# Hybrid sparse and window attention block on one core: division and lower parts on TensorE in the window branch, a new step order in the sparse branch, counting in both, mix from the first half

## The chip, the core and the metric

The kernel runs on one core of a Trainium2 chip, in one launch. The metric is the device time of that core in microseconds (us). Three runs of the kernel before give a median of 1457.87 us. The engines are TensorE (PE in the profile; PEld is its weight load), VectorE (DVE), ScalarE (ACT), GpSimd (POOL) and SyncE (SP), whose queue issues the DMAs.

## The reference

A decoder block over 1024 positions of width 1024, in float32. Two attention branches work on the same normalised input and are mixed by gates; an MLP follows.

```python
h = rmsnorm(x, attn_norm_w)
a_q, a_k, a_v, i_q, i_k, i_w, b_q, b_k, b_v, g_a, g_b = split(h @ w_in)
# a: sparse branch, per block of 128 queries
score = sum_h i_w[t,h] * relu(i_q[t,h] . i_k[s])        # 8 index heads, causal
sel   = top_k(score, 256)                                # 256 keys for each query
o_a   = softmax(a_q . a_k[sel] / 8) @ a_v[sel]           # 8 heads in 2 groups
# b: window branch, keys t-127..t, with one sink logit per head
o_b   = softmax([b_q . b_k / 8, sink])[:-1] @ b_v
mix = sigmoid(g_a) * (o_a @ w_branch_a) + sigmoid(g_b) * (o_b @ w_branch_b)
x = x + mix @ w_out
u = relu(rmsnorm(x) @ w_up); x = x + (u * u) @ w_down
out = rmsnorm(x)
```

## The kernel before

**Split products.** Every product whose operands have to be exact to float32 is made of three products of rounded operands: `mm3` (lines 110 to 115) multiplies upper by upper, upper by lower and lower by upper part. `split` (99 to 108) makes the parts: the upper one is a rounding copy (line 103 on ScalarE), the lower one the difference of source and upper part (line 108 on VectorE or GpSimd).

**Stages.** The program loads the input, begins the first gates, projects index keys and values, and computes the index scores of the blocks 2 to 7 (the blocks 0 and 1 have no more than 256 keys, so nothing is selected there). Then come the window branch `b`, the sparse branch `a`, the mix of both (`attended`, `mixed`), the product with `w_out` (tiles `pso`) and the MLP (tiles `pu`, `pdx`, `pdy`) as fast matrix products of seven block products each.

**A step** is one head group (of two, four heads each) and one block of 128 queries. Each branch has sixteen. A window step has the keys of its block and of the one before, 256 columns (128 in block 0); a sparse step of block n has all 128(n+1) columns, masked by the selection (`bias`). `attention_parts` (819 to 896) runs a step in two halves of two heads. `scores`: two products per head into a bank `S` of 512 columns (line 835; there are two banks), VectorE adds the mask and takes the row's maximum (851), ScalarE makes the exponential and its sum (854), VectorE the reciprocal of the sum (858), and then the probabilities are divided: by VectorE in the window branch (866), by GpSimd in the sparse branch (862). `apply`: for each pair of key blocks, four transposes by TensorE into a bank `pt` (877, three banks), then `split` into upper and lower part (103 on ScalarE, 108 on VectorE), then two products for each key block into the bank `pv` (882 with the upper, 883 with the lower part). At the end ScalarE copies `pv` out (890) and two stores go to DRAM (894) through SP's queue.

**Queries.** `Unit` projects the queries of a pair of blocks (tiles `mm`, lines 112 to 114, 256 columns; two times 24 products), rotates them (440, 441) and rounds them (403, 455). The four query weights are loaded and split ahead by `Columns`, on GpSimd.

**Counting.** The 256th largest score of a query is found by bisection over the bits of its float: in each round every query's row is counted against a candidate, and the candidate's next bit follows. ScalarE counts the blocks 2 to 4 (`below`, 676; VectorE compares and sets the bits, 739 to 742), VectorE the blocks 5 to 7 (674, and 736, 737 with GpSimd's 735). `bits(kind, n)` issues n rounds, `thresholds` the last one. `select(b)` (766 to 780) then makes the mask of block b. In the window branch each step ends with one round of ScalarE and two of VectorE (`RATE`, lines 923 to 928); what is left of both comes before the first sparse step.

**What sets the order.** The lines are written in a software pipeline (`pipeline`, from 466): the second half of a step's work is written `DEPTH` parts behind the first, projections `AHEAD` of it. The gates are fillers: `FILL` says for every step of a stage how many half gates (24 products of 512 columns into tiles `gt` with the copy 291 to `z_d`) are written behind it. A scheduler (`schedule_with_timeline_sim`) then sets the order of each engine's instructions. `A_ORDER` gives the order of blocks of the sparse branch: group 0 takes 1, 0, 5, 4, 7, 3, 6, 2, then group 1 takes 6, 7, 5, 0, 4, 1, 3, 2. The probabilities of a step lie in a `Ring` (`pB`, `pA`), and a step isn't begun before its place is free.

**Mix.** `attended(half, brs)` (954 to 964) loads a half of the positions of a branch's output (first the last stores, `ZLATE`), adds its two parts and splits; `mixed(half, ft, ...)` (967 to 988) loads the gates, makes the sigmoid and multiplies (975 to 985). The second half of the positions is mixed first, the first half `SKEW` = 2 tiles behind.

## Time and profile before

| | |
|---|---|
| median of 3 runs | 1457.87 us (1457.07 to 1458.74) |
| profiled execution | 1457.79 us, span 1455.9 us |
| TensorE busy | 1373.5 us (94%) |
| VectorE busy | 1072.9 us (74%) |
| ScalarE busy | 783.0 us (54%) |
| GpSimd busy | 450.9 us (31%) |
| granted TensorE clock, mean | 0.987 |

The span is the time from the first to the last instruction in the trace; the rest of the profiled execution's time lies around it. Busy time is the time in which an engine had at least one instruction under way. TensorE's instructions overlap, so a busy stretch of it can hold more or fewer products. The shares are means over stages with different limits: the index stage ends at 237 us, the window branch lies from there to 433, the sparse branch to 621, the mix to 741 and the rest behind it.

### The profile page before, as it was taken

The page shows a single profiled execution, that of the slowest core. Times are in us where ns is not written, and L with a number is a line of the kernel's source. Part 1 is how long each engine was busy: PE and PEld are TensorE (multiplying, and loading weights), DVE is VectorE, ACT ScalarE, POOL GpSimd, SP SyncE. Part 2 cuts the span into 40 slices and gives each one's busy share as a digit, 9 for nine tenths or more (in the row PEclk, how much of TensorE's full clock was granted, in tenths as well). Part 3 has the DMA queues.
Part 4 walks back from the last instruction along what each step waited for, and adds up shares of the span by engine and source line. Part 5 has one row for each costly group of instructions (what it writes and reads, how often), then busy time and mean ns, then how long its engine had stood idle before and what let it go on. Part 6 is the DMA issues. An engine that isn't in the chain of part 4 may idle for free.

```text
span 1455.9 us, 21190 instructions
## 1 busy us (share of the span) xinstructions
PE 1373.5 (94%) x7096; PEld 1164.7 (80%) x7096; DVE 1072.9 (74%) x2115; ACT 783.0 (54%) x1612; POOL 450.9 (31%) x447
## 2 busy tenths in 40 slices
PE   7999997888789899979999999999999999999998
PEld 6998886767688788867788878888888888888887
DVE  8667799999998984887553686566664697687674
ACT  6335445666676474864445576555554554445453
POOL 4463766564647554443525310000000000001001
PEclk9999998999999999999999999999999999999999
DMA  7321232232323022185556466444443988632313
GB/s 266 111 70 52 64 116 64 74 90 51 96 61 86 23 54 63 45 258 197 166 146 195 126 207 210 142 149 151 157 147 108 332 285 286 224 102 87 123 59 116
DMA packets 135245, 195.04 MB, mean 134 GB/s; under 512 B 15968, under 2 KB 59104, under 8 KB 135008
## 3 DMA queue, kind: packets, MB, share of 16 engines
q1 hardware_dynamic: 134992, 193.69, 41.7%
q8 instruction: 56, 0.92, 0.3%
q14 instruction: 53, 0.43, 0.1%
q10 hardware_dynamic: 144, 0.00, 0.0%
HBM read 130.99 MB, written 55.84 MB: 128 GB/s over the span
## 4 chain that ended last, share of the span: by engine, by line
PE 59%; DVE 23%; DMA 7%; issue 4%; ACT 4%; POOL 2%; SPq 1%; DVEq 0%; ACTq 0%; POOLq 0%
DVE of_a L674 7%; PE pu L1112 7%; PE pu L1113 7%; PE pu L1114 7%; PE pdx L1311 3%; PE pdx L1309 3%; PE pdx L1310 3%; PE pdy L1309 2%; PE pdy L1311 2%; PE pdy L1310 2%; DVE wide L851 2%; PE pso L112 2%; PE pso L113 2%; PE pso L114 2%; PE S L835 2%
## 5 line engine op out<-in xcount | busy, mean ns | idle before, releaser
L1256 POOL TENSOR_TENSOR y<-x,gf 128x512 f32<-128x512 f32 x4 | 6.3, 1604 | 493.8 <-DVE x L1240 493.8
L103 ACT ACTIVATE dao<-da 128x512 fp32r<-128x512 f32 x112 | 69.8, 630 | 126.1 <-PE pdx L1311 61.7
L112 PE MATMUL mm<-of_h,of_w 128*128 128x256 f32 x416 | 120.4, 291 | 0.0
L113 PE MATMUL mm<-of_h,of_w 128*128 128x256 f32 x416 | 119.6, 289 | 0.0
L114 PE MATMUL mm<-of_h,of_w 128*128 128x256 f32 x416 | 119.5, 289 | 0.0
L854 ACT ACTIVATE wide<-wide,of_a 128x257 f32<-128x257 f32 (+9 forms) x128 | 81.0, 634 | 65.4 <-DVE of_a L851 64.4
L108 DVE TENSOR_TENSOR dao<-da,dao 128x512 fp32r<-128x512 f32 x112 | 77.3, 695 | 40.7 <-ACT dao L103 40.7
L674 DVE TENSOR_SCALAR_CACHE_REDUCE of_a<-wide,of_a 128x768 bf16<-128x768 bf16 (+5 forms) x93 | 106.1, 1141 | 0.9
L1112 PE MATMUL pu<-XT,uo 128*128 128x512 f32 x256 | 99.9, 390 | 0.8 <-ACT snap L1145 0.8
L1113 PE MATMUL pu<-XT,uo 128*128 128x512 f32 x256 | 99.7, 390 | 0.0
L1114 PE MATMUL pu<-XT,uo 128*128 128x512 f32 x256 | 99.5, 389 | 0.0
L112 PE MATMUL gt<-of_h 128*128 128x512 f32 x224 | 91.2, 407 | 7.0 <-ACT of_h L334 7.0
L1310 PE MATMUL pdx<-dbo,dao 128*128 128x512 f32 x248 | 95.5, 390 | 0.0
L1309 PE MATMUL pdx<-dbo,dao 128*128 128x512 f32 x248 | 95.5, 390 | 0.0
L1311 PE MATMUL pdx<-dbo,dao 128*128 128x512 f32 x248 | 94.0, 390 | 0.5 <-DVE dao L108 0.5
L676 ACT ACTIVATE of_a<-uall,of_a 128x384 int8<-128x384 f32 (+2 forms) x93 | 66.8, 718 | 51.2 <-DVE of_a L742 31.4
L835 PE MATMUL S<-of_w 128*128 128x256 f32 (+3 forms) x320 | 79.8, 342 | 14.9 <-DVE of_a L851 14.8
L114 PE MATMUL gt<-of_h 128*128 128x512 f32 x224 | 91.2, 408 | 2.4 <-POOL of_h L108 2.4
L113 PE MATMUL gt<-of_h 128*128 128x512 f32 x224 | 91.1, 407 | 0.9 <-DVE of_h L335 0.9
L877 PE MATMUL pt<-kept,wide 128*128 128x128 f32 x408 | 68.4, 278 | 17.8 <-DVE wide L866 8.8
L113 PEld LDWEIGHTS mm<-of_h,of_w 128*128 128x128 f32 x416 | 81.9, 197 | 1.0
L112 PEld LDWEIGHTS mm<-of_h,of_w 128*128 128x128 f32 x416 | 81.7, 197 | 0.8
(284 smaller groups left out, 4298.4 us busy)
## 6 DMA issues: line engine op xcount, KB each, us to landing
u_d<-u SPq DMA_DIRECT2D x112, 256.0 KB, 2.2
da<-u_d SPq DMA_DIRECT2D x112, 256.0 KB, 4.5
ur<-in_w_up_dram SPq DMA_DIRECT2D x32, 512.0 KB, 4.7
dr<-in_w_down_dram SPq DMA_DIRECT2D x64, 256.0 KB, 5.3
z_d<-of_g SPq DMA_DIRECT2D x32, 256.0 KB, 2.2
uall<-z_d SPq DMA_DIRECT2D x32, 256.0 KB, 3.5
raw<-in_w_out_dram SPq DMA_DIRECT2D x32, 256.0 KB, 4.5
of_g<-in_w_g_dram SPq DMA_DIRECT2D x28, 256.0 KB, 2.8
```

The lines of the kernel that those rows point to most:

```text
L112: ins = nc.tensor.matmul(ps, lhsT=ah, rhs=bh, start=first, stop=False)
L113: nc.tensor.matmul(ps, lhsT=ah, rhs=bl, start=False, stop=False)
L114: nc.tensor.matmul(ps, lhsT=al, rhs=bh, start=False, stop=last)
L674: nc.vector.tensor_scalar(j, src, c, None, op0=ALU.is_lt, op1=ALU.add, accum_out=a)
L835: marks["S"] = nc.tensor.matmul(pS[:, :e - c], lhsT=st.unit(b, j), rhs=kT[:, a, k0 + c:k0 + e], start=a == 0, stop=a == 1).ins
L854: nc.scalar.activation(pe, pe, AF.Exp, bias=last, scale=-1.0, accum_out=st.sm[:, j:j + 1])
L1112: nc.tensor.matmul(ps, lhsT=ah, rhs=xh[:, at], start=f0, stop=False, skip_group_check=True)
L1113: nc.tensor.matmul(ps, lhsT=ah, rhs=xl[:, at], start=False, stop=False, skip_group_check=True)
L1114: nc.tensor.matmul(ps, lhsT=al, rhs=xh[:, at], start=False, stop=last, skip_group_check=True)
L1309: nc.tensor.matmul(ps, lhsT=ah[:, js], rhs=x[0][:, at], start=first, stop=False, skip_group_check=True)
L1310: nc.tensor.matmul(ps, lhsT=ah[:, js], rhs=x[1][:, at], start=False, stop=False, skip_group_check=True)
L1311: nc.tensor.matmul(ps, lhsT=al[:, js], rhs=x[0][:, at], start=False, stop=end, skip_group_check=True)
```

## The change

*Window branch.* The division by the sum leaves the probabilities: the loop of line 862 to 866 runs for the sparse branch alone. The output is multiplied instead: for each of the four heads TensorE transposes the reciprocal, broadcast along the row, into a bank `rb`, and VectorE multiplies the copied output by it. The lower part of the transposed probabilities is made by TensorE and ScalarE: behind the transposes in bank `pt` ScalarE copies the upper part out, TensorE adds to the bank the product of the upper part with the negative identity (`minus`), and ScalarE copies out what is left, the lower part.

*Sparse branch.* The order of the steps is a list of (group, block): it begins with the blocks 1, 0, 3, 2 of group 0, goes through all eight of group 1 and ends with 6, 7, 5, 4 of group 0. The query weight of group 0 is loaded and split a second time for the last four steps. VectorE's rounds of counting alternate between two and one in the window steps, and eight more rounds are written into the first seven sparse steps. `select` comes at the first use of a block, from the step ahead. The ring of the sparse branch ends ahead of `topall`, which VectorE's counting still reads, until the last step is begun.

*Mix.* The first half of the positions is mixed first, the second half behind it. The buffers for it lie in another part of `uall`. *Fillers:* `FILL` has other numbers of half gates per step.

```diff
-FILL = {'i': '000000000000', 'b': '0222000000010110', 'a': '1101110011011111'}
+FILL = {'i': '000000000000', 'b': '0222011001010101', 'a': '1111011010101010'}
...
-A_ORDER = [[1, 0, 5, 4, 7, 3, 6, 2], [6, 7, 5, 0, 4, 1, 3, 2]]
+A_STEPS = [(0, 1), (0, 0), (0, 3), (0, 2), (1, 1), (1, 0), (1, 3), (1, 2), (1, 5), (1, 4), (1, 7), (1, 6), (0, 6), (0, 7), (0, 5), (0, 4)]
+BITS = {'b': '2121212121212121', 'a': '1111112'}
...
     ident = kept(P)
     make_identity(nc, ident)
+    minus = const.tile([P, P], F32R, name="minus")
+    nc.vector.tensor_scalar(minus, ident, -1.0, None, op0=ALU.mult)
...
             nc.vector.reciprocal(inv, inv)
-            for j in range(j0, j0 + 2):
+            for j in range(j0, j0 + 2) if st.name == "a" else ():
...
                 ph, pl = att["ph"](), att["pl"]()
-                split(ph[:, :m], pl[:, :m], pt[:, :m], "act")
+                if st.name == "b":
+
+                    nc.scalar.copy(ph[:, :m], pt[:, :m])
+                    nc.tensor.matmul(pt[:, :m], lhsT=minus, rhs=ph[:, :m], start=False, stop=True, skip_group_check=True)
+                    nc.scalar.copy(pl[:, :m], pt[:, :m])
+                else:
+                    split(ph[:, :m], pl[:, :m], pt[:, :m], "act")
...
-            if EVAC == "a":
+            if st.name == "b":
+
+                rb = bank("tr", [P, R, P], "rb")
+                for j in range(R):
+                    nc.tensor.transpose(rb[:, j], st.sm[:, j:j + 1].to_broadcast([P, P]), ident)
+                nc.scalar.copy(o, st.pv)
+                nc.vector.tensor_tensor(o, o, rb, ALU.mult)
+            elif EVAC == "a":
                 nc.scalar.copy(o, st.pv)
...
         bits("act", RATE["act"])
-        bits("dve", RATE["dve"])
+        bits("dve", int(BITS['b'][i]))
...
-    pA = Ring(wide)
+    pA = Ring(wide, wide_spent)
+    more = Columns(I["w_aq"][0], 2, 256, "pool", "pool", tag="p")
+    steps = [Step(g, b, more if i >= 12 else wq[2 + g], kT=akT[g], v=av[g], kb=(0, b + 1), sink=False, p=pA, dst=o_d["a"],
...
     bits("act", RATE["a"] - done["act"])
-    bits("dve", 32)
...
     def begin(i):
+        if i == NB:
+            pA.end = wide.shape[1]
         if i:
             bits("act", RATE["late"])
-        if i == 0 and steps[0].b in IDX_BLOCKS:
-            select(steps[0].b)
-        if i + 1 < NB and steps[i + 1].b in IDX_BLOCKS:
-            select(steps[i + 1].b)
+        bits("dve", int(BITS['a'][i:i + 1] or 0))
+        for st in steps[i:i + 2]:
+            if st.b not in ready:
+                ready.add(st.b)
+                select(st.b)
...
-    attended(1, "ba")
-    attended(0, "b")
+    attended(0, "ba")
+    attended(1, "b")
...
-            mixed(1, i, *ws[i])
+            mixed(0, i, *ws[i])
         if i == 0:
-            attended(0, "a")
+            attended(1, "a")
         if i >= SKEW:
-            mixed(0, i - SKEW, *ws[i - SKEW])
+            mixed(1, i - SKEW, *ws[i - SKEW])
```

What stands on the engines, at three places. First TensorE in the ninth window step, before. `gt` are gate products (lines 112 to 114), `pt` transposes (877), `S` scores (835), `pv` products with the values (882).

```order
L114 MATMUL gt<-of_h 128x512
L112 MATMUL gt<-of_h 128x512
L877 MATMUL pt<-kept,wide 128x128
L113 MATMUL gt<-of_h 128x512
L877 MATMUL pt<-kept,wide 128x128 x3
L114 MATMUL gt<-of_h 128x512
L112 MATMUL gt<-of_h 128x512
L113 MATMUL gt<-of_h 128x512
L835 MATMUL S<-of_w 128x128
L882 MATMUL pv<-of_w 128x256
L835 MATMUL S<-of_w 128x128 x3
```

TensorE in the same step, after. Scores are line 839 now, transposes 881, the products with the negative identity 886, products with the values 892 and 893, and 903 are the transposes of the reciprocal.

```order
L839 MATMUL S<-of_w 128x128 x4
L886 MATMUL pt<-of_w,minus 128x512
L881 MATMUL pt<-kept,wide 128x128 x4
L839 MATMUL S<-of_w 128x128 x4
L893 MATMUL pv<-of_w 128x256
L892 MATMUL pv<-of_w 128x256
L893 MATMUL pv<-of_w 128x256
L892 MATMUL pv<-of_w 128x256
L881 MATMUL pt<-kept,wide 128x128 x4
L903 MATMUL rb<-kept,of_a 128x128 x4
```

The gate products are gone from this step, and the new product (886) and the four transposes of the reciprocal (903) stand between scores and products with the values.

Second, TensorE among the large blocks of the sparse branch, before (block 5 of group 1).

```order
L835 MATMUL S<-of_w 128x256 x2
L877 MATMUL pt<-kept,wide 128x128 x3
L883 MATMUL pv<-of_w 128x256
L882 MATMUL pv<-of_w 128x256
L883 MATMUL pv<-of_w 128x256
L882 MATMUL pv<-of_w 128x256
L877 MATMUL pt<-kept,wide 128x128 x4
L835 MATMUL S<-of_w 128x512 x2
```

The same engine after (block 6 of group 1).

```order
L839 MATMUL S<-of_w 128x384 x2
L893 MATMUL pv<-of_w 128x256
L892 MATMUL pv<-of_w 128x256
L893 MATMUL pv<-of_w 128x256
L114 MATMUL gt<-of_h 128x512
L115 MATMUL gt<-of_h 128x512
L113 MATMUL gt<-of_h 128x512
L114 MATMUL gt<-of_h 128x512
L881 MATMUL pt<-kept,wide 128x128
L115 MATMUL gt<-of_h 128x512
L113 MATMUL gt<-of_h 128x512
L839 MATMUL S<-of_w 128x512 x2
```

Gate products (113 to 115 now) stand among the products of the large blocks, where none stood.

Third, ScalarE at the end of the window branch, before. 676 are its counts, 854 exponentials, 103 upper parts, 403 rounded queries, 435 the copy of a projection.

```order
L676 ACTIVATE of_a<-uall,of_a 128x384
L103 ACTIVATE of_w<-pt 128x512
L854 ACTIVATE wide,of_a<-wide,of_a 128x257
L676 ACTIVATE of_a<-uall,of_a 128x512
L435 COPY of_a<-mm 128x512
L854 ACTIVATE wide,of_a<-wide,of_a 128x256
L103 ACTIVATE of_w<-pt 128x512
L676 ACTIVATE of_a<-uall,of_a 128x640
L890 COPY of_a<-pv 128x512
L854 ACTIVATE wide,of_a<-wide,of_a 128x256 x3
```

ScalarE at the same place, after. Counts are line 680, copies of upper and lower part 885 and 887, of `pv` 904.

```order
L904 COPY of_a<-pv 128x512
L680 ACTIVATE of_a<-uall,of_a 128x640
L887 CAST of_w<-pt 128x512
L680 ACTIVATE of_a<-uall,of_a 128x384
L680 ACTIVATE of_a<-uall,of_a 128x512
L887 CAST of_w<-pt 128x512
L680 ACTIVATE of_a<-uall,of_a 128x640
L885 CAST of_w<-pt 128x512
L680 ACTIVATE of_a<-uall,of_a 128x384
L438 COPY of_a<-mm 128x512
L680 ACTIVATE of_a<-uall,of_a 128x512
```

Counts now stand in a row there, with the copies of upper and lower parts between them, where before exponentials of the first sparse steps stood between single counts.

## Rows read from the trace of the kernel before

**Rows 1.** Busy tenths in 40 slices of 36.4 us, the page's part 2.

```profile
PE   7999997888789899979999999999999999999998
DVE  8667799999998984887553686566664697687674
```

**Rows 2.** Stretches: length, busy PE, PEld, DVE, ACT, POOL (instructions), clock, DMA share, GB/s.

```profile
237.00:433.00 196.00, 162.92 (x1034) 142.14 (x1033) 189.90 (x557) 131.37 (x357) 102.53 (x145) 0.97 0.29 75
433.00:621.00 188.00, 176.28 (x1120) 155.83 (x1118) 147.33 (x363) 114.22 (x251) 105.24 (x101) 0.98 0.22 58
621.00:741.00 120.00, 106.47 (x480) 86.03 (x481) 86.03 (x128) 58.61 (x99) 54.73 (x43) 0.97 0.62 195
900.00:920.00 20.00, 20.00 (x90) 16.55 (x89) 12.72 (x20) 10.42 (x19) 0.00 (x0) 1.00 0.47 164
```

**Rows 3.** Timeline, PE: start, duration (us), line, operation, count, idle before.

```profile
236.78 0.33 PE L835 MATMUL S<-of_w 128*128 128x128 f32 x2
...
433.60 0.28 PE L113 MATMUL mm<-of_h,of_w 128*128 128x256 f32 x1
433.72 0.28 PE L114 MATMUL mm<-of_h,of_w 128*128 128x256 f32 x1
...
456.92 0.63 PE L835 MATMUL S<-of_w 128*128 128x512 f32 x2
...
621.04 0.62 PE L835 MATMUL S<-of_w 128*128 128x384 f32 x2 [1.01 <-DVE of_a L851]
...
741.33 0.39 PE L112 MATMUL pso<-mixall,wh 128*128 128x512 f32 x1
```

**Rows 4.** Groups by form, DVE, 236 to 452 us: busy us, mean ns, idle before.

```profile
L866 DVE TENSOR_SCALAR wide<-wide,of_a 128x256 f32<-128x256 f32 x56 | 25.4, 494 | 0.1
L674 DVE TENSOR_SCALAR_CACHE_REDUCE of_a<-wide,of_a 128x1024 bf16<-128x1024 uint16 x16 | 20.3, 1271 | 0.0
L108 DVE TENSOR_TENSOR of_w<-pt,of_w 128x512 fp32r<-128x512 f32 x29 | 19.8, 683 | 1.5 <-ACT of_w L103 1.5
L674 DVE TENSOR_SCALAR_CACHE_REDUCE of_a<-wide,of_a 128x896 bf16<-128x896 uint16 x16 | 18.2, 1137 | 0.1
L674 DVE TENSOR_SCALAR_CACHE_REDUCE of_a<-wide,of_a 128x768 bf16<-128x768 uint16 x16 | 16.2, 1010 | 0.1
...
L866 DVE TENSOR_SCALAR wide<-wide,of_a 128x128 f32<-128x128 f32 x8 | 3.0, 409 | 0.0
```

**Rows 5.** Groups by line, whole span: GpSimd's division and weight splits, VectorE's gate product.

```profile
L862 POOL TENSOR_SCALAR wide<-wide,of_a 128x256 f32<-128x256 f32 (+7 forms) x64 | 51.6, 820 | 68.5 <-DVE of_a L858 46.4 <-PE S L835 14.5 <-PE pt L877 4.8
L108 POOL TENSOR_TENSOR of_w<-of_a,of_w 128x512 fp32r<-128x512 f32 x32 | 45.6, 1432 | 2.4 <-PE trk L526 1.3
...
L984 DVE TENSOR_TENSOR uall<-psy,uall 128x512 f32<-128x512 f32 x32 | 21.6, 686 | 24.8 <-ACT uall L977 24.1 <-PE psy L114 0.6
```

**Rows 6.** Groups by line, ACT, 236 to 452 us.

```profile
L676 ACT ACTIVATE of_a<-uall,of_a 128x640 int8<-128x640 f32 (+2 forms) x82 | 59.0, 719 | 33.1 <-DVE of_a L742 25.2 <-DVE of_a L858 7.2
...
L103 ACT ACTIVATE of_w<-pt 128x512 fp32r<-128x512 f32 (+1 forms) x33 | 18.4, 557 | 0.3 <-PE pt L877 0.3
L676 ACT ACTIVATION_READ_ACCUMULATOR of_a<-uall,of_a 128x1 f32 x82 | 15.5, 188 | 0.0
```

**Rows 7.** Waits of PE, 600 to 690 us: total us, times, longest.

```profile
PE pv L883 <- DVE of_w L108: 5.0, 5, 1.8
PE psy L112 <- ACT wh L103: 3.6, 1, 3.6
```

**Rows 8.** Timeline at 329 us: POOL and DVE.

```profile
329.52 1.29 POOL L108 TENSOR_TENSOR of_h<-of_g,of_h 128x512 fp32r<-128x512 f32 x1
...
330.06 0.77 DVE L739 TENSOR_TENSOR of_a<-of_a 128x3 int32<-128x3 f32 x1
```

**Rows 9.** Instructions of line 866: shortest, median and longest in ns.

```profile
L866 DVE TENSOR_SCALAR wide<-wide,of_a x64: 275/348/1442, 249.1 to 440.8; 128x256 f32<-128x256 f32 x56, 128x128 f32<-128x128 f32 x8
```

**Rows 10.** Tile `S`: what ended idle time of PE before its products (us, times).

```profile
  DVE of_a L851: 34.6, 36
```

## What the change should do to the time

> **What bounds the kernel now.** I read the busy tenths of the page first [rows 1]. From the nineteenth slice of 36.4 us to the last but one TensorE (PE) is at 9; the holes lie before, and in slices seven to fourteen VectorE (DVE) stands at 9 in all but one, while PE stands at 7 or 8 in all but one. The stretches say it in numbers [rows 2]: in the window branch (237 to 433 us) DVE is busy 189.90 of 196 us and PE 162.92; in the sparse branch (433 to 621) PE is busy 176.28 of 188 and DVE 147.33; in the mix (621 to 741) PE 106.47 of 120. Busy PE is not PE at its pace, because its instructions overlap: in a saturated stretch 90 products of 512 columns fill 20.00 us, about 0.227 us each [rows 2], and products of 256 columns start 0.12 us apart [rows 3]. So VectorE sets the end of the window branch, TensorE that of the sparse branch, and the change takes work from VectorE and puts some of it on TensorE.
>
> **How I priced it.** Every instruction in the order of the old and of the new program got the mean duration of its kind in this trace (on DVE less the 0.07 us by which neighbours overlap; PE's at its pace), and I summed them engine by engine between the marks of PE's first score product of each step (a step is one head group by one block of 128 queries). For the old program I took per step the engine with most work: 189.9 us for the first fifteen window steps, 25.1 for the next three, 84.1 for the next six, 75.0 for the last seven before the last step. The sum is 374.0. Measured, from the first window score at 236.8 to the last step's first score at 621.0, it is 384.2 [rows 3]; the split at 456.9 gives 220.1 against 215.0 and 164.1 against 159.1. So this sum holds within 3% on both sides of the split.
>
> **Part by part.** *Division.* 64 products by the reciprocal leave DVE: 56 of 0.494 us and 8 of 0.409 [rows 4] are 30.9, less overlap 26. Instead 16 products of the output by a transposed reciprocal come in: the nearest row is 0.686 us for 512 columns with one input in PSUM [rows 5], so 16 x 0.62 = 10. TensorE gets 64 transposes of 128 columns, each under the 0.12 us of a 256 column product: 7.
>
> *Lower parts.* 28 subtractions of 512 columns at 0.683 us [rows 4] and 4 of 256 leave DVE: less overlap 18. TensorE gets 28 x 0.227 + 4 x 0.12 = 6.8, ScalarE 32 copies at 0.557 [rows 6], 17.8. In place of ScalarE then VectorE, each pair of blocks now goes ScalarE, TensorE, ScalarE. TensorE waits for the upper part in its queue, and behind it stand scores and the next step's query products; VectorE waits for those scores. What this hand-over costs no row of before shows: between nothing, where VectorE's queue of 1.0 to 1.27 us counts [rows 4] is what it escapes (that could be a gain), and about 1 us for each of the 32, the hand-over of a count (25.2 us over 27 rounds, 0.93 [rows 6]), if the products always stall. I take nothing beyond the few per cent that the old sums lack, since TensorE has most slack just there.
>
> *Counting.* A round of VectorE is three counts, 1.27 + 1.14 + 1.01 us [rows 4], and two small ones. In the new order the counting in the first fifteen window steps falls from 94.5 to 77.0 us, and 19.5 stand among the first sparse blocks. Nothing is saved, 17.5 is moved. ScalarE's rounds (three counts, 0.72 us each plus 0.19 to read the sum [rows 6], handed over to VectorE each time) are moved too: of the 26 after the first window score 23 ran in the fifteen window steps before, 14 do now; 12 instead of 3 stand in the next three steps.
>
> *What moved with it.* The scheduler fills TensorE differently. Counted in the two orders, in the fifteen window steps stood 217 gate products and 432 query products; now 73 and 288, so 144 x 0.227 + 144 x 0.12 = 50 us of TensorE's work leaves the stretch in which it had slack. It comes back as 65 more gate products in the next three steps and 54 more gate and 84 more query products in the last seven steps, where TensorE is the bound already.
>
> *Sums of the new order*, us, TensorE, VectorE, ScalarE: fifteen window steps 98.0, 126.3, 115.5 (before 138.6, 189.3, 128.6); next three 49.2, 32.8, 52.7 (24.5, 19.2, 22.5); next six 65.5, 64.7, 30.5 (77.8, 78.3, 49.6); last seven 109.0, 82.6, 73.1 (69.4, 50.6, 51.1). Largest engine per step and summed: 142.0 + 59.3 + 70.1 + 116.4 = 387.8, against 374.0: the window branch gains 48, the rest loses 62. But the new order counts two rounds in one window step and one in the next, and puts gates into every second step, so that its steps change their largest engine in turn. What one engine is behind in one step it can partly make up in the next, if the others lead. Taken over pairs of steps (the mean of both ways to cut) the sums are 369.7 old and 380.0 new, over threes 367.6 and 371.5. Scaled so that the old one gives the measured 384.2, the new order costs 14.2 more by single steps, 10.7 by pairs, 4.1 by threes. I take the middle of pairs and threes, 7: the order says in which step a count stands, not how far the engines are apart.
>
> *At nothing or nearly.* The reload of one query weight: four loads of 256 KB on SP's queue, where the DMA share is 0.22 [rows 2], and four splits on GpSimd of at most 2 x 1.43 us [rows 5], 11 us; its cover is that GpSimd is busy 105.24 of 188 us there; without it the last two query projections would start up to 11 us late. The negative identity is one instruction in the start. *Mix from the first half*: the last blocks are then large ones of the second half, and all of the first half's inputs are there before. From the last step's first score to the first output product the old program took 120.3 us [rows 3] for 98.7 us of products, the new one has 101.1. Of the waits there [rows 7], 5.0 us of products for lower parts on DVE can be filled by mix products, which now stand among them; the 3.6 us for branch weights stay, since those are loaded behind the last store in both. I take 2.4 - 5 = -3, between -5 and +4.
>
> A rule on two engines bears on the moved counts. The row first: a VectorE comparison of three columns took 0.77 us, beginning while a GpSimd subtraction ran and ending 0.02 us after it [rows 8]; the divisions by reciprocal took between 275 and 1442 ns [rows 9]. The Trainium skill (SBUF — State Buffer, section Who interferes with whom) says that VectorE and GpSimd share a port pair that an instruction with two inputs in SBUF, or in a two-port mode, holds or waits for as a whole; the trace agrees (0.77 us). It speaks for taking the divisions off VectorE and against counting beside GpSimd's divisions of the sparse branch. My sums hold such waits at their mean.
>
> **The rivals.** A, the forecast: TensorE's fillers move into its bound stretch and take back a little more than VectorE gave. 7 from the steps less 3 in the mix makes +4: 1457.8 + 4 = 1462 us, 1459 to 1472 with single steps (14.2 - 3) at its upper end and threes (4.1 - 3) at its lower.
>
> B, faster: the engines even out over many steps. Taking the largest engine only over the four stretches gives 353.5 for the new order against 361.5 for the old; scaled by 384.2/361.5 that is 375.7, -8.5, and -3 in the mix: 1446 us, 1438 to 1455 (below, if the products for lower parts escape VectorE's queue). For it: VectorE is relieved by 26 + 18 - 10 = 34 us. Against it: the score products wait for VectorE's reductions of the banks two before, 34.6 us over 36 waits [rows 10], so a step's lead is short; and in the old program the sum by steps fits better than the one by stretches (3% against 6%). The Trainium skill (Perfetto Trace Analysis, section Optimizing Scalar/DVE Operations) says that where VectorE is saturated, work moved to ScalarE may help; by that rule this is the case that comes.
>
> C, slower still: ScalarE's twelve rounds become the chain. A round's own work is 3 x (0.72 + 0.19) = 2.7 us plus 0.93 of hand-over, 3.7, and 12 of them 44 us, inside the 59.3 of that stretch. But in the window branch a round took 216 / 27 = 8 us. From 59.3/12 = 4.9 us a round on, the chain decides, since the first selected block waits for its last round; at 6 us it is 72, 13 more. Up to ten small instructions of VectorE's moved rounds meeting a GpSimd division of 0.82 us [rows 5] add up to 8. With A's 4 that is 1475 to 1490.
>
> D, no change: the 48 gained in the window branch and what is lost behind it cancel: 1455 to 1460. That the change doesn't do what it says I leave out: the order shows the instructions gone.
>
> **How the numbers follow.** The profiled execution took 1457.79 us, its span 1455.9; the median of the runs is 1457.87, so differences carry over as they are. Chances: A 0.36, B 0.34, C 0.13, D 0.17. What a measurement can tell from no change is 0.2%, 2.9 us, so the lowest part of A (0.02) counts as no change: faster 0.34, same 0.19, slower 0.47. The predicted time is A's, 1462. The range 1443 to 1480 takes in A, D, most of B and a third of C; its ends contain the unknown hand-over of the 32 products (0 to 30 us, in part covered) and the mix's -5 to +4. Cases of both signs hold most of the chance; A's own range is 1459 to 1472.
>
> **What would show it.** Right: the window branch ends some 40 us earlier, VectorE below 95% busy in it, the granted clock no higher; ScalarE in a row of counts with TensorE on gates behind it; the stretch with blocks 4 to 7 longer than before with TensorE at its pace; first output product 2 to 10 us later. Wrong, towards B: first sparse score 50 us or more earlier while the last seven steps take under 105 us. Wrong, towards C: the first selected block's scores waiting for VectorE's selection while TensorE idles over 5 us there.

## The result, and the profile after

The changed kernel takes 1490.03 us (median of 4 runs, 1488.7 to 1491.71) against 1457.47 us, a ratio of 1.0224 (95% interval 1.0211 to 1.0237). That is 32.6 us slower, where 4 us were forecast and 1480 was the upper end of the range. The profiled execution took 1489.98 us, its span is 1487.9 us against 1455.9.

The busy tenths of the page after, now in slices of 37.2 us; they answer to [rows 1].

```profile
PE   7999998877996999988999999999999999999998
DVE  8666899999358985596563666656655598686774
ACT  6335436778874445565345566555555544444453
PEclk9999998889998999999999999999999999999999
```

VectorE's row of nines is shorter, as it should be with work taken from it. TensorE's row isn't fuller for that: it has a 6 in the thirteenth slice, where it had a 9 or an 8, and its clock shows 8 in four slices.

The stretches after, cut where the prediction cut them: fifteen window steps, next three, next six, last seven, and the last step's first score to the first output product (columns as in [rows 2]).

```profile
235.00:385.30 150.30, 121.11 (x754) 107.86 (x752) 132.16 (x390) 110.78 (x301) 81.29 (x122) 0.88 0.26 68
385.30:437.90 52.60, 50.62 (x335) 45.48 (x333) 23.56 (x71) 43.86 (x113) 25.98 (x28) 1.00 0.36 91
437.90:529.30 91.40, 74.33 (x430) 64.98 (x429) 81.77 (x188) 39.74 (x104) 58.49 (x58) 0.91 0.23 61
529.30:650.70 121.40, 113.71 (x721) 99.62 (x720) 84.23 (x194) 68.69 (x130) 61.96 (x52) 1.00 0.26 72
650.70:772.00 121.30, 107.62 (x498) 87.10 (x497) 81.48 (x125) 55.98 (x93) 47.42 (x37) 0.97 0.54 171
```

The same five stretches of the kernel before.

```profile
236.80:425.80 189.00, 156.09 (x979) 135.52 (x977) 184.98 (x543) 124.18 (x337) 100.68 (x143) 0.96 0.28 74
425.80:456.90 31.10, 27.37 (x189) 25.33 (x188) 23.78 (x63) 25.33 (x71) 20.49 (x24) 0.95 0.28 69
456.90:546.40 89.50, 83.20 (x534) 73.91 (x533) 81.77 (x178) 47.95 (x97) 52.98 (x44) 0.98 0.21 53
546.40:621.00 74.60, 72.74 (x458) 63.41 (x456) 46.90 (x139) 48.13 (x106) 33.81 (x37) 1.00 0.23 63
621.00:741.30 120.30, 106.77 (x481) 86.27 (x482) 86.33 (x128) 58.61 (x99) 54.73 (x43) 0.97 0.62 194
```

The window steps gain 39 us. The next three stretches lose 22, 2 and 47, and the tail 2 (its output product begins at 772.9 us, before at 741.3); behind that both kernels take 715. The granted clock is 0.88 in the window steps (0.96 before) and 0.91 in the six steps from the first selected block on (0.98).

What stands at the seam shows in the timeline after: ScalarE's last round of counting, VectorE's selection of block 3, its first reduction with that selection, and ScalarE's exponential behind it (start and duration in us).

```profile
445.95 0.62 ACT L680 ACTIVATE of_a<-uall,of_a 128x384 int8<-128x384 f32 x1 [3.04 <-DVE of_a L746]
...
449.19 0.83 ACT L680 ACTIVATE of_a<-uall,of_a 128x640 int8<-128x640 f32 x1
...
464.10 0.72 ACT L858 ACTIVATE wide<-wide,of_a 128x512 f32<-128x512 f32 x1 [7.50 <-DVE of_a L855]
```

```profile
454.39 0.48 DVE L778 TENSOR_SCALAR of_a<-uall,of_a 128x512 bf16<-128x512 f32 x1
454.90 1.23 DVE L780 TENSOR_TENSOR_SCAN of_a<-kept,of_a 128x512 bf16<-128x512 f32 x1
...
459.90 1.64 DVE L784 SCALAR_TENSOR_TENSOR uall<-uall,of_a 128x512 f32<-128x512 f32 x1
...
463.38 0.68 DVE L855 CUSTOM_DVE_ANT_0 wide<-S,uall 128x512 f32<-128x512 f32 x1
```

And the waits of the kernel after from 437 to 470 us (total, times, longest).

```profile
PEld mm L113 <- DVE of_a L855: 9.5, 1, 9.5
ACT wide L858 <- DVE of_a L855: 9.3, 3, 7.5
PE mm L113 <- DVE of_a L855: 9.2, 1, 9.2
```

The window steps end 40 us earlier (the last one's first score at 385.3, before at 425.8), yet the first block with a selection begins its reductions at 463.4 us, before at 459.6. The blocks that the new order takes first are those that ScalarE counts, and its last round starts only at 445.95 (before at 453.5, but there a block that VectorE counts goes first). In between TensorE does gate and query products, then stands for 9.2 us.

### The profile page after: what moved, and what is told of

It is laid out like the page before. It is cut to its first block, busy times and chain, and to the rows that moved or that the text cites. A ratio compares the mean times of both kernels' runs of the same rounds, so it can differ in the third digit from the quotient of the medians.

```text
span 1487.9 us, 21308 instructions
## 1 busy us (share of the span) xinstructions
PE 1393.9 (94%) x7192; PEld 1184.7 (80%) x7192; DVE 1055.1 (71%) x2036; ACT 798.1 (54%) x1644; POOL 463.0 (31%) x455
## 5 line engine op out<-in xcount | busy, mean ns | idle before, releaser
L113 PE MATMUL mm<-of_h,of_w 128*128 128x256 f32 x416 | 123.2, 297 | 9.8 <-DVE of_a L855 9.8
L115 PE MATMUL mm<-of_h,of_w 128*128 128x256 f32 x416 | 122.9, 295 | 2.3 <-POOL of_w L109 2.3
L114 PE MATMUL mm<-of_h,of_w 128*128 128x256 f32 x416 | 121.8, 293 | 0.0
L858 ACT ACTIVATE wide<-wide,of_a 128x257 f32<-128x257 f32 (+9 forms) x128 | 81.4, 638 | 67.5 <-DVE of_a L855 66.7
L113 PEld LDWEIGHTS mm<-of_h,of_w 128*128 128x128 f32 x416 | 84.3, 203 | 11.5 <-DVE of_a L855 9.5
L115 PEld LDWEIGHTS mm<-of_h,of_w 128*128 128x128 f32 x416 | 83.6, 201 | 4.0 <-POOL of_w L109 2.8
L114 PEld LDWEIGHTS mm<-of_h,of_w 128*128 128x128 f32 x416 | 84.0, 202 | 1.4
```

Of the source, the lines that this page charges most:

```text
L113: ins = nc.tensor.matmul(ps, lhsT=ah, rhs=bh, start=first, stop=False)
L114: nc.tensor.matmul(ps, lhsT=ah, rhs=bl, start=False, stop=False)
L115: nc.tensor.matmul(ps, lhsT=al, rhs=bh, start=False, stop=last)
L858: nc.scalar.activation(pe, pe, AF.Exp, bias=last, scale=-1.0, accum_out=st.sm[:, j:j + 1])
```

## The experiments

Two theories stood first. **Chain:** the sparse branch waits for ScalarE's rounds, which the shorter window steps don't bring forward. **TensorE:** its new products (28 x 0.227 + 4 x 0.12 + 64 x 0.062 = 10.8 us at the pace of [rows 2, 3], 0.062 being about half the pace of 256 columns; the expectations say 14, from the forecast's 6.8 + 7) and its lower clock. A third, VectorE's rounds among the first sparse blocks, is named in the first expectations; A and B in the later ones are told there. The table has every run: time, ratio with its interval, and from its trace the first reduction with a selection, the TensorE work then left up to the first output product (products counted, 0.227 us for 512 columns and in proportion, 0.062 for 128), and the start of that product. The trace is of one execution, up to 5.5 us off the median (e9 1483.8, e10 1470.7, e8 1472.9 us), and behind the output product the runs take 714 to 725 us, so its column doesn't give the time by itself.

| run | us | ratio | first selected | work left | output product |
|---|---|---|---|---|---|
| before | 1457.5 | 1 | 459.6 | 226.1 | 741.3 |
| after | 1490.0 | 1.0224 [1.0211, 1.0237] | 463.4 | 241.7 | 772.9 |
| e1 | 1487.1 | 1.0197 [1.0179, 1.0216] | 460.6 | 235.9 | 761.7 |
| e2 | 1482.8 | 1.0171 [1.0148, 1.0194] | 473.4 (block 4) | 235.9 | 760.4 |
| e3 | 1455.9 | 0.9992 [0.9980, 1.0003] | 455.5 | 217.3 | 734.9 |
| e4 | 1489.2 | 1.0212 [1.0193, 1.0231] | 463.1 | 238.6 | 768.4 |
| e5 | 1474.7 | 1.0129 [1.0110, 1.0147] | 445.2 | 253.1 | 753.8 |
| e6 | 1458.0 | 1.0007 [0.9997, 1.0017] | 460.3 | 220.8 | 740.8 |
| e7 | 1479.9 | 1.0159 [1.0141, 1.0176] | 454.7 | 235.7 | 761.2 |
| e8 | 1469.2 | 1.0090 [1.0071, 1.0108] | 458.0 | 226.6 | 746.5 |
| e9 | 1478.2 | 1.0155 [1.0130, 1.0180] | 476.9 | 218.0 | 761.9 |
| e10 | 1474.5 | 1.0125 [1.0105, 1.0146] | 476.6 | 217.3 | 753.8 |
| e11 | 1458.6 | 1.0017 [1.0007, 1.0027] | 456.7 | 221.1 | 742.5 |
| e12 | 1467.4 | 1.0072 [1.0055, 1.0089] | 462.3 | 221.4 | 749.2 |
| e13 | 1500.9 | 1.0300 [1.0284, 1.0315] | 478.4 | 250.1 | 782.4 |
| e14 | 1498.0 | 1.0280 [1.0263, 1.0297] | 468.1 | 252.1 | 775.5 |
| e15 | 1466.7 | 1.0065 [1.0050, 1.0081] | 454.4 | 217.3 | 747.7 |
| e16 | 1455.4 | 0.9987 [0.9978, 0.9996] | 455.3 | 217.3 | 736.5 |

**e1, two rounds of ScalarE in each window step.**

```diff
-RATE = {'dve': 2, 'act': 1, 'a': 32, 'late': 2}
+RATE = {'dve': 2, 'act': 2, 'a': 32, 'late': 2}
```

> The kernel after, with two rounds of ScalarE's counting instead of one in each window step. Theory 1 (the chain of ScalarE's rounds: in the trace after its last round starts at 446.0 us and the first selected block's reduction comes at 463.4, as late as before, 459.6, though the window steps end 39 us earlier): the rounds end some 30 us earlier, the first selected block comes at 435 to 450, and the time falls to 1465 to 1480. Theory 2 (TensorE's own work: 14 us more products, and a granted clock of 0.88 in the window branch instead of 0.96): nothing of that changes, 1486 to 1494. Theory 3 (VectorE's rounds among the first sparse blocks): the same as theory 2.

1487.05 us. The edit didn't bring about what it was meant to: ScalarE's rounds begin within 1 us of the same times up to 370 us, and the last begins at 446.3, as after. The scheduler had not been held by the place of the lines. It decides nothing between the theories.

**e2, the window part alone; e3, everything but the window part.** For e2 the diff's pieces at `minus`, the division, the lower part and `rb` are put into the kernel before; for e3 they are taken out of the kernel after.

> The kernel before, with the division and the lower parts of the window branch as in the change; steps of the sparse branch, counting, fillers and mix as before. Theory 1: VectorE's queue is shorter, so that ScalarE's rounds, one a window step, end earlier as well, and counting on VectorE bounds the window branch: 1445 to 1458. Theory 2: 14 us of products more, TensorE has 44 us idle before 621 us which takes some of it: 1462 to 1475. Theory 3: the sparse part stays as it was, 1440 to 1456.

> The kernel after with division and lower parts in the window branch as before: order of the sparse branch, counting, fillers and mix as after. Theory 1: the window branch takes some 20 us more, in which ScalarE's rounds go on, so that they end no later than 455 us: 1485 to 1495. Theory 2: 14 us of products fewer: 1474 to 1480. Theory 3: counting among the first sparse blocks stays: 1480 to 1495.

e2 is 25 us slower than before, e3 is not different from before. So the loss belongs to the window part, and the sparse part, counting, fillers and mix together cost nothing: e3's output product begins 6.4 us earlier than before, and what stands behind it takes 6.1 longer. VectorE's rounds among the first sparse blocks are still in e3, which rules the third theory out as a cause by itself. In e2 the window steps end 30 us earlier and block 5, which VectorE counts, begins at 423.6; then block 4 waits for ScalarE's rounds until 473.4. e2 shows that wait, but TensorE is busy 30.4 us of the 33 from 440 to 473, and the time is far above what I had expected of the chain and 8 us above what the TensorE theory allowed; e3 is faster than any of them had it.

e3 also shows what the wait costs by itself. Its block 3 waits from its first score at 436.1 us to its first reduction at 455.5, and TensorE has products for all of the 19.4 us; in the kernel after it waits 25.5 us, and TensorE is busy in 17.5 of them. First e3, then after:

```profile
436.10:455.50 19.40, 19.40 (x136) 17.98 (x135) 16.69 (x40) 8.36 (x21) 18.19 (x17) 1.00 0.44 110
```

```profile
437.87:463.38 25.51, 17.53 (x105) 14.88 (x103) 18.06 (x43) 11.00 (x29) 14.11 (x14) 0.95 0.28 72
```

**e4, the fillers of before.** `FILL` as in the kernel before.

> The kernel after with the gates as filler at the steps of before (the table FILL of before). Theory 1: TensorE has gates in the window steps again and lacks them while it waits for ScalarE's rounds; the first selected block still comes at 455 to 470: 1485 to 1500. Theory 2: the clock in the window steps comes back to 0.95 or more, 1475 to 1485. Theory 3: 1486 to 1494.

1489.16 us: as after. The table of fillers alone isn't the cause.

**e5 and e6, without ScalarE's last eight rounds,** in the kernel after and in the kernel before.

```diff
-        if bit < -1:
+        if bit < -1 or kind == "act" and 0 <= bit < 8:
             return
```

> The kernel after without the last eight of ScalarE's rounds of counting and VectorE's settings behind them, so that the thresholds of blocks 2 to 4 are coarser than the reference's. Theory 1 (in every variant so far the first selected block's reduction came at 455 to 473 us, whenever the window steps ended, because ScalarE's rounds end only then; TensorE has less of its old work done by then than before, since ScalarE does 18 us more and its rounds come 10 to 13 us apart in the window steps): the rounds end some 40 us earlier, the first selected block comes at 420 to 435, the time falls to 1455 to 1470. Theory 2 (TensorE's 14 us of new products and its clock): the 21 us of ScalarE's work aren't on the path, 1483 to 1492.

> The kernel before without the last eight of ScalarE's rounds of counting, as in the run on the kernel after. Theory 1: VectorE, busy 97% of the window steps, bounds them here, and ScalarE's rounds end only 20 us behind them: 1440 to 1452, a smaller gain than in the kernel after. Theory 2: 1452 to 1460.

After, 15.3 us come back (1490.03 to 1474.71), less than the chain theory had and more than the TensorE theory; before, none, with the same counts taken from ScalarE. The chain is on the path in the kernel after and not in the kernel before, whose order takes blocks counted by VectorE first. But it is under half of the loss, and the first selected block came 18 us earlier, not 30 to 40: the last round begins at 403.3 us, and TensorE's queue has its gates and projections in front of the first sparse scores. The mask of block 3 is ready at 423.9 there, TensorE's first score of it comes at 439.2. In e9, e10, e13 and e14 below it is the same, the mask 14 to 41 us ahead of the score (e13: 433.1 and 474.5). So the chain is off the path in them, and e5, e9 and e10 still take 18.5 to 22.3 us more than e3: that rest is no wait for the chain's end.

**e7, the lower parts copied out by VectorE; e8, the lower parts as before and the division on TensorE.**

```diff
-                    nc.scalar.copy(pl[:, :m], pt[:, :m])
+                    nc.vector.tensor_copy(pl[:, :m], pt[:, :m])
```

> The kernel after with the lower parts still made by TensorE but copied out of the bank by VectorE instead of ScalarE, 32 copies. Theory 1: ScalarE has 18 us less before its last round, the first selected block comes 8 to 18 us earlier: 1470 to 1482. Theory 2: the same products on TensorE, 1484 to 1494; VectorE, with 18 us more, could add to it, up to 1500.

> The kernel after with the lower parts as before, by VectorE from the bank; the division stays on TensorE. Theory 1: 18 us less on ScalarE and no hand-over to TensorE and back: 1465 to 1478, near to e3 by more than half of the 34 us. Theory 2: 7 us of products fewer of 14: 1478 to 1484.

From e3 to e8 the division costs 13.3 us, from e8 to after the lower parts 20.8 (the other order wasn't tried); 10.1 of these come back when VectorE copies instead of ScalarE. That fits the chain: ScalarE's 18 us of copies stand in the queue of its counts, and without them the last round begins at 439.0 us instead of 446.0 and the first selected block at 454.7 instead of 463.4. The waits at the hand-over itself are short. The products of line 886 after, with what they waited for and who waited for them (us, times):

```profile
L886 PE MATMUL pt<-of_w,minus x32: 280/396/502, 252.7 to 409.5; 128*128 128x512 f32 x28, 128*128 128x256 f32 x4
its engine sat idle before it (us, times) until:
  ACT of_w L885: 1.6, 3
who waited for it (us, times):
  ACT of_w L887: 2.2, 3
```

**e9, more fillers in the window steps and fewer in the sparse ones; e10, with all of VectorE's rounds there too; e11 and e12, the same two edits apart, without the window part.**

```diff
-FILL = {'i': '000000000000', 'b': '0222011001010101', 'a': '1111011010101010'}
+FILL = {'i': '000000000000', 'b': '0222111111111111', 'a': '1111000000000000'}
```

```diff
-BITS = {'b': '2121212121212121', 'a': '1111112'}
+BITS = {'b': '2222222222222222', 'a': ''}
```

> The kernel after with one half gate as filler behind every window step from the fourth on and one behind each of the first four sparse steps; in the order 24 gate products stand in each of the window steps 9 to 14 where none or few stood. Theory A (while ScalarE's rounds end at 440 to 455 us anyway, TensorE has gaps, its granted clock falls, and old work is left for behind the selection; span times missing clock is 35.7 us after against 18.9 before and 17.5 without the window part): the clock loss falls to 25 to 30, 25 us more of gates are done before the first selected block, and the time falls to 1468 to 1480. Theory B (VectorE bounds the sparse part, 257 us busy of 309 between the first selected block and the first output product): less to fill its waits with, 1485 to 1495.

> As the run with more fillers, and all of VectorE's rounds of counting in the window steps as before, two in each. Theory A: the window steps are longer by some 17 us but ScalarE's rounds end no later, TensorE has gates there: 1462 to 1478. Theory B: 30 us of VectorE's work leave the sparse part and the time falls by 15 us or more against the run with more fillers alone.

> Without division and lower parts on TensorE (as in the third run), with these fillers. Theory A: VectorE's queue is as full as before in the window steps, TensorE's clock is 0.98 there already and nothing is to be had: 1452 to 1460. Theory B: fewer gates among the sparse blocks, where VectorE bounds: 1452 to 1460 as well; a time under 1450 would speak against both.

> Without division and lower parts on TensorE (as in the third run), with all of VectorE's rounds in the window steps. Theory A: window steps 17 us longer, as in the kernel before; 1453 to 1462. Theory B: the sparse part is shorter by some 20 us, the window part longer by 17: 1450 to 1456.

In the kernel after the fillers give back 11.8 us and the early counts 3.8 more (the intervals of the two runs overlap; theory B had 15 or more), with 24 us less work left behind the selection than after, though the first selected block comes 13 us later. Without the window part the fillers cost 2.7 (against e3) and the early counts 11.4, more than either theory had. So the kernel after has room in its window steps that its order doesn't use, and the kernel without the window part has none.

**e13, the room filled; e14, the same without the window part.** Twelve products that nobody reads are written into each window step. The scheduler put 48 of the 192 ahead of the first window score, in both runs, and the rest between there and 421 us (e13) and 406 (e14). They use the banks of the gates, so what a gate waits for such a bank is in the result too.

```diff
+            if st.name == "b" and j0:
+                dm = bank("gt", [P, 512], "dummy")
+                for k in range(12):
+                    nc.tensor.matmul(dm, lhsT=hT[0, k % KT][0][:, :P], rhs=hT[0, k % KT][1], start=k == 0, stop=k == 11)
```

> The kernel after with twelve products of 512 columns in each window step that nobody reads (their result is left in a bank), 192 products or 43.6 us of TensorE's work at its pace; nothing is left out. Theory A1 (the lower granted clock in TensorE's gaps is itself what costs): the clock in the window steps rises from 0.84 to 0.95 or more, the time without the clock loses some 10 us less, and the time falls to 1478 to 1486 although 43.6 us of work are added. Theory A2 (the gaps cost because old work is left for later; the clock follows from them): nothing is gained, the products take room, 1490 to 1510. Theory B (neither; VectorE's and ScalarE's hand-overs set the window steps): 1488 to 1494.

> The same 192 products added where division and lower parts are as before (the third run's kernel, 1455.94 us), in which TensorE has 57 us unused or at the lower clock up to the first selected block. Theory A1: the clock is 0.98 there already, the products cost 5 to 25 us: 1461 to 1481. Theory A2: they take the room of gates and query products, 1465 to 1490. Theory B: VectorE sets the steps, 1454 to 1462.

43.6 us of products cost 10.9 us in the kernel after and 42.1 in e3's, which is above what any theory had for e14. In both ScalarE's last round begins earlier (415.9 and 413.7 us) without gain. In e14 34.8 us of gates and query products moved from ahead of the first selection to behind it (252.1 left against 217.3). The stretch from 300 to 350 us, after, e13, e3 and e14:

```profile
300.00:350.00 50.00, 38.20 (x260) 35.43 (x258) 48.63 (x140) 36.23 (x98) 24.78 (x44) 0.86 0.22 46
```

```profile
300.00:350.00 50.00, 42.93 (x268) 38.10 (x267) 49.00 (x145) 34.23 (x94) 22.75 (x43) 0.93 0.21 50
```

```profile
300.00:350.00 50.00, 40.81 (x250) 33.83 (x249) 49.93 (x140) 32.97 (x89) 27.75 (x40) 1.00 0.29 77
```

```profile
300.00:350.00 50.00, 42.42 (x253) 36.31 (x254) 49.76 (x140) 32.90 (x91) 23.07 (x35) 0.95 0.23 60
```

In e13 the clock comes up from 0.86 to 0.93 there (over the execution from 0.976 to 0.986), and the time still rises by 10.9 us: the higher clock doesn't pay for the products that brought it. Across the table the output product comes late where much work is left at the first selection, or where that is late, but loosely: from the sum of the two columns to the third there are 51 to 71 us (e15, with another mix, 76), a spread of more than half the loss.

**e15, the mix of e3 from the second half; e16, the first half's last tile moved behind the second half's.** In e15 the three places of the diff in the mix are as before; in e16 the pairs run ... (0, 6), (1, 6), (1, 7), (0, 7).

> The third run's kernel with the mix from the second half first as before. The last steps of the new order are blocks of the second half, so that the first products of the mix would wait for the last store: 1458 to 1470 if the order of the mix gives what its own part takes away at the output product (6.4 us earlier at the first output product than before, 6.5 us lost in that product's stage); 1453 to 1457 if it makes no difference.

> The third run's kernel with the last tile of the first half moved behind the last tile of the second half in the mix. The output product begins with the second half, whose last tile is the last thing made in the kernel after; there TensorE waits 3.1 us and its clock stands at 0.83 for 20 us in the third run. With another tile behind it: 1449 to 1453; if the wait is only moved into the mix: 1454 to 1458.

With the new order of steps the old order of the mix costs 10.8 us. e16 is 0.13% faster than before (0.04 to 0.22%), the best of the runs and within 0.5 us of e3; in the first 20 us of the output product TensorE is busy 18.70 us at a clock of 1.00, in e3 16.85 at 0.83, but the product begins 1.6 us later.

## Why the prediction was wrong

The direction was right, the size short by 28 us. The direction is in part luck: the forecast never priced the window part apart from the rest, and e2 and e3 show that the part it had as the relief (34 us off VectorE) loses 25 us alone, while the rest loses nothing. By its own terms:

- **Instructions.** Sizes held: the products for lower parts are 32, the copies behind them take 0.554 us (0.557 forecast), the multiplications 0.682 (0.686). The hand-over, open between 0 and 30 us, is 1.6 + 2.2 us of waits.
- **Sums by steps.** The stretches came to 150.4, 52.6, 91.4 and 121.4 us, 415.8 together, against 142.0, 59.3, 70.1 and 116.4. The step that failed is to sum the busiest engine of each step with no term for a wait between steps. The term where it shows is the third, the six steps behind the first selected block's first score: 21 us short. They were priced by their own work, while the first selected block stands 25 us in them (437.9 to 463.4) and waits for ScalarE's rounds and the selection, and TensorE is idle for 17.1 of the 91.4 us. About half of the 21 stands in e3 too, which has the same order of blocks, a wait of 19.4 us and 81.4 us for these six steps. I had seen the twelve rounds and made them rival C, but let them decide only above 4.9 us a round, inside a stretch that was to be long anyway. They took 5.0 (389.6 to 450.0), and VectorE's thresholds and selection, 13 us from 450 to 463, stand behind them: these I had not put on the chain.
- **Window steps.** 8 us short. VectorE was busy 132.16 us where I had summed 126.3, and I priced TensorE at its pace where its clock was 0.88; which of the two made them longer isn't shown.
- **Evening out.** Pairs and threes of steps took the forecast down from 14.2 to 7. The measured difference is 31.6 (415.8 - 384.2): nothing evened out, and single steps were the best of the three.
- **"TensorE has most slack just there."** This is the wrong premise under the lower parts. [rows 2] has TensorE idle 33 of 196 us, but e14 shows that room taken in the order of e3: of 43.6 us of added products 34.8 push other work behind the selection.
- **Mix.** -3 forecast, +1.9 measured from the last step's first score to the first output product (122.2 against 120.3), inside its bounds; e15 shows that the new order of steps needs it.
- **Slips in the working.** A's upper end, single steps less 3, is 1469 and not 1472. The trace has 28 rounds of ScalarE behind the first window score where I counted 26: 24 and 4 before, 16 and 12 after, the last two of the 12 in the third stretch. Neither changes the forecast.

Together: 17.4 us beyond the scaled single steps, 7.2 of evening out, 4.9 in the mix, 0.4 behind it, less 1.9 by which the first score came earlier, make the 28.

Of the marks set: VectorE fell to 132.16 of 150.3 us (88%), the clock was no higher, ScalarE counted in a row beside gates, the last seven steps were long (121.4), as said. The mark of rival C, the first selected block waiting for the selection while TensorE idles over 5 us, was met too (9.2 us). Rival B's mechanism, VectorE relieved and work on ScalarE, was seen in the window steps alone: the Trainium skill's rule (Perfetto Trace Analysis, section Optimizing Scalar/DVE Operations) speaks for a stretch in which VectorE is saturated, and there 39 us were had; the stretches behind lost more than that again, up to 15.3 us of it by ScalarE, on which a serial count ran until 450 us.

**What stays open.** The runs account for the loss by parts (13.3 division, 20.8 lower parts) and show the chain (15.3); what the rest is, is argued. The division alone costs 13 us where its new products are 4. In e8 9.3 us more work is left behind the selection than in e3 (226.6 and 217.3), which fits displaced work, yet which line of the order makes it wasn't tried. The stretch from the first window score to the output product says something of it (before, e2, e3, e8, after):

```profile
236.80:741.30 504.50, 446.17 (x2634) 384.44 (x2633) 423.75 (x1045) 304.20 (x706) 262.69 (x288) 0.97 0.34 97
235.10:760.40 525.30, 466.18 (x2730) 405.94 (x2729) 394.49 (x960) 317.11 (x737) 263.32 (x287) 0.95 0.33 93
235.60:734.90 499.30, 443.15 (x2634) 379.07 (x2633) 427.30 (x1043) 301.48 (x705) 276.12 (x296) 0.98 0.35 99
236.10:746.50 510.40, 453.68 (x2698) 393.19 (x2697) 417.81 (x995) 303.64 (x706) 271.99 (x296) 0.97 0.34 97
234.90:772.90 538.00, 468.39 (x2730) 405.82 (x2730) 404.20 (x965) 319.79 (x738) 275.23 (x296) 0.94 0.33 93
```

Length less busy PE is TensorE's idle time: 58.3, 59.1, 56.2, 56.7 and 69.6 us. So e2 is longer than before, and e8 longer than e3, with hardly more idle time, by 20.8 and 11.1 us; they have 10.8 and 4.0 us more products and stand at the lower level of the clock for 51 us against 27 and 34 against 17. There the TensorE theory fits better than the chain; of the five only the kernel after idles more, 13 us above e3. That the lower clock itself costs these microseconds isn't shown: e16, the fastest, stands at the lower level for 44 us of its stretch.

## What to carry to other kernels

Where fillers run beside a bound engine, an idle share of TensorE needn't be free room: add useless work there and see what it costs before anything real is moved in. Relieving the engine that bounds a stretch helps only as far as the next stretch can use the time; look for a serial chain on another engine that ends at a time of its own, and take out a part of it to test. A wait for such a chain costs what the other engines can't fill: in e3 TensorE had products for all 19.4 us of it. Copies moved onto the engine that carries the chain cost 10.1 us here.

## What the hardware showed that I had not expected

TensorE's granted clock fell and rose within tens of microseconds where its work came in bursts with gaps between. Four slices of the kernel after (columns as above):

```profile
305.00:315.00 10.00, 6.23 (x31) 5.74 (x32) 9.86 (x29) 7.27 (x20) 4.22 (x9) 0.66 0.26 56
315.00:325.00 10.00, 9.21 (x76) 8.80 (x74) 9.61 (x26) 8.46 (x22) 5.20 (x11) 1.00 0.17 36
325.00:335.00 10.00, 7.38 (x37) 7.02 (x38) 9.24 (x33) 7.48 (x24) 4.06 (x5) 0.66 0.24 49
335.00:345.00 10.00, 8.60 (x69) 8.05 (x69) 9.95 (x25) 6.42 (x18) 3.97 (x8) 1.00 0.17 36
```

In the third, products of 256 columns start 0.21 to 0.22 us apart and take 0.41, at the end of it 0.12 and 0.28, the two levels of 1.2 and 2.4 GHz; ahead of them stand two waits for VectorE, the first of them 2.05 us:

```profile
326.26 0.39 PE L892 MATMUL pv<-of_w 128*128 128x256 f32 x1 [2.05 <-DVE of_a L855]
...
328.81 1.12 PE L881 MATMUL pt<-kept,wide 128*128 128x128 f32 x4 [1.37 <-DVE of_a L855]
...
331.00 0.41 PE L893 MATMUL pv<-of_w 128*128 128x256 f32 x1
331.22 0.41 PE L892 MATMUL pv<-of_w 128*128 128x256 f32 x1
...
334.72 0.28 PE L115 MATMUL mm<-of_h,of_w 128*128 128x256 f32 x1
334.84 0.28 PE L113 MATMUL mm<-of_h,of_w 128*128 128x256 f32 x1
```

The same four slices before stand at 1.00, 1.00, 1.00 and 0.83 with TensorE busy 34.94 of 40 us, against 31.42 after. Over the whole execution the mean clock was 0.976 after and 0.987 before.
